# A two-layer backbone on one core: the first product of both MLPs by Strassen's algorithm, pairs of unit blocks at a time

## The chip, the cores and the metric

The kernel runs on one core of a Trainium2 chip. The metric is the time of one execution on the device, in microseconds (us). A kernel's time is the median over several executions; a profile is one further execution, recorded by the hardware. TensorE (PE) does the matrix products, with its weight loads (PEld) beside them; VectorE (DVE), ScalarE (ACT) and GpSimd (POOL) work on vectors; SyncE (SP) starts most transfers.

## The reference

Latent tokens (1024 of width 1024) and 256 context tokens pass two layers. Layer 0 mixes with a bidirectional state-space scan (SSD) beside neighbourhood attention (NA), layer 1 with a short gated convolution. Each layer ends in an MLP. This is the part that matters here:

```python
def sq_relu_mlp(h, w1, w2):
    return jnp.square(jax.nn.relu(h @ w1)) @ w2

...
        x = x + gate_a * y
        h = modulate(rmsnorm(x, norm_mlp_w[i]), shift_f, scale_f)
        x = x + gate_f * sq_relu_mlp(h, mlp_w1[i], mlp_w2[i])
    return rmsnorm(x, final_norm_w)
```

`w1` is 1024 x 4096 and `w2` 4096 x 1024, all in float32. `modulate` is `h * (1 + scale) + shift`, with vectors that come from a product of the conditioning vector with `mod_w`.

## The kernel before

Everything is kept transposed: channels on the 128 partitions, tokens along the free axis, in two halves t = 0 and 1 of 512 tokens. `x[t][k]` is the residual stream's block row k (of 8) of half t.

Each float32 product is three passes of a faster format. A value is split into a high part (a cast on ACT) and a low part (value minus high part, on DVE); the product is wh·xh + wh·xl + wl·xh, three matmuls of a 128 x 128 weight block with 512 columns, summed in PSUM. The class `Weights` does this for weights, in the order of a queue, `srcs`: a transfer on SP's queue into `wf` (128 x 512, two buffers), the cast to `wh` (L69) and the subtraction to `wl` (L70), four buffers each. `prefetch(n)` keeps n of them ready, `take` hands them out. `split` is the same pair of operations for activations. Each engine runs its instructions in the order in which they stand for it; a scheduler sets that order from the program's order and priorities when the kernel is built.

The program's stages are: norm and input projection (to about 120 us), SSD and NA with the output projection (to about 1220), MLP 0 (to about 1925), the short-convolution mixer (to about 2280), MLP 1 (to about 2990), final norm. In an MLP, the 32 blocks of 128 hidden units go in 8 groups of 4. For each block and half, `gemm` makes 24 matmuls (8 block rows of channels by three passes) into a PSUM bank `g`, ACT takes the relu and the high part of its square, DVE squares (L1094) and subtracts to get the low part (L1095). Then `proj` makes the second product of the group: for 8 output blocks and 2 halves 12 matmuls each into a `g`, and `resid` adds it to the stream, `x<-g,modv,x` (L883, on DVE). Five banks serve `g` and three `r`, for small sums.

The norm ahead of a stage has parts that are called as hooks inside the previous product: per half, a sum over partitions by a matmul with ones (`rstd`, L124, then small steps on DVE with a power on POOL, to `dg`), a broadcast by a matmul with `dg` (L141), and for each block row three operations: `xr` (L155, DVE), high part `hh` (L156, ACT), low part `hl` (L157, DVE). `acc` is the running sum of squares (L146 to L150). `mod_cols` computes the modulation vectors of layer 1, 128 columns in a step of 8 DVE operations (`macc`, L181 and L183): 48 steps, called as `between()` in MLP 0.

At the program's end, `fin1`, `fin2`, `fin3` are the final norm for three pieces of tokens (half 0, and two quarters of 256), with a scaling (L1193) and a transfer out for each block row.

## Time and profile before

| what | before |
|---|---|
| three runs, median (lowest to highest) | 3009.93 us (3008.55 to 3010.86) |
| profiled execution, its own time | 3005.5 us |
| its span (first to last instruction) | 3003.6 us |
| TensorE, mean granted clock | 0.997 of full |
| matmuls recorded | 14232 |
| busy: PE, PEld, DVE, ACT, POOL | 2940.2, 2416.9, 1739.0, 1042.9, 327.6 us |

The span leaves out about 2 us around the first and last instruction. The profiled execution is 4.4 us quicker than the median of the three timed runs. Busy time of the matmuls comes from modelled ends, since they are pipelined; the distance between starts tells the pace.

### The profile page before, as it was taken

How to read it: one execution, taken by the hardware profiler on the slowest of the kernel's cores; microseconds unless marked ns; L12 is line 12 of the kernel's file. 1: busy time of each engine (PE TensorE's matmuls, PEld its weight loads, DVE VectorE, ACT ScalarE, POOL GpSimd, SP SyncE). 2: the span in 40 equal slices, each digit the busy share in tenths (PEclk: the TensorE clock that was granted, in tenths of full speed). 3: DMA queues.
4: the chain of work that ended last, by engine and by line, in shares of the span. 5: the costliest groups of instructions: out<-in, count | busy, mean ns of one | idle time of the engine just before them, and what ended most of it. 6: DMA issues, size and time to landing. Idle time of an engine off the chain costs nothing.

```text
span 3003.6 us, 38877 instructions
## 1 busy us (share of the span) xinstructions
PE 2940.2 (98%) x14232; PEld 2416.9 (80%) x14232; DVE 1739.0 (58%) x3681; ACT 1042.9 (35%) x2006; POOL 327.6 (11%) x320
## 2 busy tenths in 40 slices
PE   8999999999999999999999999999999999999998
PEld 4888777777888778788888888788887888888886
DVE  6766758758998863755555554733336333333336
ACT  3544335446666642321212222422223222222222
POOL 1000024425545300000000000000000000000000
PEclk9999999999999999999999999999999999999999
DMA  7256765557776652223333331111111111111112
GB/s 215 88 193 205 252 164 149 161 147 186 203 177 167 180 174 62 67 88 90 90 91 91 89 90 55 36 57 50 43 56 43 50 50 50 47 48 50 47 49 78
DMA packets 333807, 317.09 MB, mean 106 GB/s; under 512 B 82544, under 2 KB 249456, under 8 KB 333616
## 3 DMA queue, kind: packets, MB, share of 16 engines
q1 hardware_dynamic: 331744, 311.98, 35.8%
q8 instruction: 113, 1.85, 0.2%
q10 hardware_dynamic: 1872, 2.62, 0.2%
q14 instruction: 78, 0.64, 0.1%
HBM read 254.24 MB, written 60.29 MB: 105 GB/s over the span
## 4 chain that ended last, share of the span: by engine, by line
PE 72%; DVE 4%; DMA 2%; issue 1%; ACT 1%; POOL 1%; SPq 0%; POOLq 0%; DVEq 0%; ACTq 0%
PE g L110 22%; PE g L111 22%; PE g L112 22%; PE v L1025 2%; PE r L999 1%; PE r L978 1%; PE r L979 1%; PE r L997 1%; DMA yf<-yna 0%; DMA yf<-yssd 0%; DVE P L985 0%; DVE PT L70 0%; DVE xr L155 0%; DVE hl L157 0%; DVE P L990 0%
## 5 line engine op out<-in xcount | busy, mean ns | idle before, releaser
L110 PE MATMUL g<-hh,wh 128*128 128x512 f32 (+1 forms) x2472 | 954.4, 387 | 3.1 <-ACT hh L69 0.8
L111 PE MATMUL g<-hl,wh 128*128 128x512 f32 (+1 forms) x2472 | 944.7, 383 | 2.3 <-DVE hl L157 2.0
L112 PE MATMUL g<-hh,wl 128*128 128x512 f32 (+1 forms) x2472 | 942.7, 382 | 2.1 <-DVE wl L70 2.0
L69 ACT CAST wh<-wf 128x512 fp32r<-128x512 f32 x442 | 274.9, 622 | 944.6 <-PE g L111 927.5
L112 PEld LDWEIGHTS g<-hh,wl 128*128 128x128 f32 x2472 | 465.0, 188 | 92.2 <-DVE wl L70 5.2
L111 PEld LDWEIGHTS g<-hl,wh 128*128 128x128 f32 x2472 | 465.5, 188 | 90.4 <-DVE hl L157 6.0
L110 PEld LDWEIGHTS g<-hh,wh 128*128 128x128 f32 x2472 | 464.9, 188 | 90.1 <-issue 1.7
L110 PE MATMUL g<-ah,wh 128*128 128x512 f32 (+1 forms) x1296 | 505.3, 390 | 0.4 <-ACT ah L69 0.3
L111 PE MATMUL g<-al,wh 128*128 128x512 f32 (+1 forms) x1296 | 501.7, 387 | 0.2 <-DVE al L70 0.2
L112 PE MATMUL g<-ah,wl 128*128 128x512 f32 (+1 forms) x1296 | 501.0, 387 | 0.0
L883 DVE SCALAR_TENSOR_TENSOR x<-g,modv,x 128x512 f32<-128x512 f32 (+1 forms) x300 | 222.7, 742 | 374.9 <-PE g L112 374.6
L70 DVE TENSOR_TENSOR wl<-wf,wh 128x512 fp32r<-128x512 f32 x442 | 308.3, 699 | 204.5 <-ACT wh L69 204.0
L110 PEld LDWEIGHTS g<-ah,wh 128*128 128x128 f32 x1296 | 243.5, 188 | 51.0 <-ACT ah L69 1.6
L111 PEld LDWEIGHTS g<-al,wh 128*128 128x128 f32 x1296 | 243.5, 188 | 50.1 <-DVE al L70 1.1
L112 PEld LDWEIGHTS g<-ah,wl 128*128 128x128 f32 x1296 | 243.4, 188 | 49.2
L1094 DVE TENSOR_TENSOR relu<-relu 128x512 f32<-128x512 f32 x128 | 88.2, 690 | 232.6 <-ACT ah L1093 232.6
L183 DVE SCALAR_TENSOR_TENSOR macc<-mw,sc,macc 128x128 f32<-128x128 f32 (+1 forms) x448 | 171.4, 383 | 11.1
L989 POOL TENSOR_SCALAR P<-P,mn 128x384 f32<-128x384 f32 (+1 forms) x128 | 154.8, 1210 | 191.1 <-DVE mn L988 140.6
L1091 ACT ACTIVATE relu<-g 128x512 f32<-128x512 f32 x128 | 76.1, 596 | 254.0 <-PE g L112 253.9
L128 POOL TENSOR_TENSOR rs<-ms,neghalf 128x4 f32<-128x4 f32 (+2 forms) x20 | 16.5, 827 | 1092.0 <-DVE ms L126 1090.5
L987 ACT ACTIVATE P<-P,mn 128x640 f32<-128x640 f32 (+1 forms) x128 | 103.1, 805 | 48.2 <-DVE P L985 46.9
L70 DVE TENSOR_TENSOR PT<-r,PT 128x256 fp32r<-128x256 f32 (+1 forms) x256 | 113.6, 463 | 1.9 <-ACT PT L69 1.0
(197 smaller groups left out, 2791.9 us busy)
## 6 DMA issues: line engine op xcount, KB each, us to landing
wf<-in_mlp_w SPq DMA_DIRECT2D x256, 256.0 KB
mw<-in_mod_w SPq DMA_DIRECT2D x64, 512.0 KB
wf<-in_in_w SPq DMA_DIRECT2D x90, 256.0 KB
mw<-in_mod_w SPq DMA_DIRECT2D x16, 1024.0 KB
wf<-in_out_w SPq DMA_DIRECT2D x48, 256.0 KB
wf<-in_sc_in SPq DMA_DIRECT2D x48, 256.0 KB
...
```

Source lines behind the costliest of these rows:

```text
L69: nc.scalar.copy(hi, src)
L70: nc.vector.tensor_sub(lo, src, hi.bitcast(F32))
L110: nc.tensor.matmul(ps, wh, xh, start=first and k == 0, stop=False)
L111: nc.tensor.matmul(ps, wh, xl, start=False, stop=False)
L112: nc.tensor.matmul(ps, wl, xh, start=False, stop=last and k == n - 1)
L183: nc.vector.scalar_tensor_tensor(acc, mw[:, k], sc[:, k, 0:1], acc, op0=OP.mult, op1=OP.add)
L883: nc.vector.scalar_tensor_tensor(xk, ps[:, :n], gate, xk, op0=OP.mult, op1=OP.add)
L987: nc.scalar.activation(P[:, w0:], P[:, w0:], AF.Exp, bias=mn[:, 1:2], scale=-1.0, accum_out=mn[:, 2:3])
L989: nc.gpsimd.tensor_scalar(P[:, w0:384], P[:, w0:384], mn[:, 3:4], None, op0=OP.mult)
L1025: nc.tensor.matmul(o, l, r, start=i == 0, stop=i == len(seq) - 1, skip_group_check=True)
L1091: nc.scalar.activation(r, ps, AF.Relu)
L1094: nc.vector.tensor_mul(r, r, r)
```

## The change

Per MLP, the hidden units are taken two blocks at a time, m = 0 to 15. Pair 0 is done as before. From pair 1 on the first product is one level of Strassen's algorithm in Winograd's form. The weights of a pair are a matrix of 2 x 2 quarters (block by half of the channels: a11, a12, a21, a22), the activations one of 2 x 2 quarters (half of the channels by half of the tokens). Seven products of quarters, each 4 block rows by three passes = 12 matmuls, replace eight. They need:

- sums of weight quarters, s1 = a21 + a22, s2 = s1 - a11, s3 = a11 - a21, s4 = a12 - s2, made on POOL (`add`) from the raw tiles `yf` into `xr`, then split like other weights (`entry`, a callable in `srcs`);
- sums of activation quarters, made once per MLP by `combine(k)` for k = 0 to 3: five POOL operations, three DVE sums, four splits, into T[0] to T[3]; their buffers are `sb` (three) and `relu` (two);
- sums of products: two are formed in PSUM by going on in the same bank (`x`, `y`), others by a copy on ACT (`kept`) that DVE adds when it makes the hidden values (`hidden` with a `part`).

The second product is `second(m)`, for each pair: 16 outputs of 6 matmuls and 16 `resid`, so that there are 256 per MLP in place of 128. The weights `w2` are laid out anew for it. PSUM in an MLP is now three banks `g`, two `r`, two `x`, one `y`. Half of the `mod_cols` steps of layer 1 move from MLP 0 to the mixer. At the program's start the transfers are reordered and the first three blocks of the input projection are interleaved over k.

```diff
     def mlp_srcs(l):
-        for g in range(8):
-            for f in range(4):
-                srcs.extend(halves(a["mlp_w1"][l, g * 4 + f], 8))
-            srcs.extend(a["mlp_w2"][l, g, b] for b in range(8))
...
+        def add(x, y, op):
+            t = np_.tile([128, 512], F32, name="xr", bufs=3).rearrange("p (k c) -> p k c", k=4)
+            nc.gpsimd.tensor_tensor(t, x, y, op=op)
+            return t
...
+        for m in range(1, 16):
+            srcs.extend(entry(m, x) for x in ("s2", "s1", "s3"))
+            if m < 15:
+                srcs.append(entry(m + 1, "a11"))
+            srcs.extend(entry(m, x) for x in ("a22", "s4"))
+            if m < 15:
+                srcs.append(entry(m + 1, "a12"))
+            srcs.extend(w2(m))
...
+        def hidden(m, f, t, ps, part=None):
+            r = Tmp()
+            ah, al = Act()
+            if part is None:
+                nc.scalar.activation(r, ps, AF.Relu)
+                nc.scalar.activation(ah, r, AF.Square)
+                nc.vector.tensor_mul(r, r, r)
+            else:
+                nc.vector.tensor_add(r, ps, part)
+                nc.vector.scalar_tensor_tensor(r, r, 0.0, r, op0=OP.max, op1=OP.mult)
+                nc.scalar.copy(ah, r)
+            nc.vector.tensor_sub(al, r, F(ah))
...
+        def combine(k):
+
+            whole = []
+            for t, i in ((0, k), (1, k), (1, k + 4), (0, k + 4)):
+                v = Tmp() if len(whole) == 3 else Sum()
+                nc.gpsimd.tensor_tensor(v, F(hs[t][i][0]), F(hs[t][i][1]), op=OP.add)
+                whole.append(v)
+            x, y, z, w = whole
+            nc.vector.tensor_sub(z, z, y)
+            nc.gpsimd.tensor_tensor(y, y, x, op=OP.subtract)
+            nc.vector.tensor_add(x, z, x)
+            nc.vector.tensor_sub(w, w, x)
+            for i, v in ((2, z), (1, x), (3, w), (0, y)):
+                if i:
+                    h_, l_ = (ap_.tile([128, 512], F32R, name=n, bufs=12) for n in ("ah", "al"))
+                else:
+                    h_, l_ = H1(k, 1)
+                split(h_, l_, v)
+                T[i][k] = h_, l_
...
+        combine(0)
+        x, p1 = begin1()
+        combine(1)
+        begin2(1, p1)
+        second(0, False, {3: lambda: combine(2), 7: lambda: combine(3)})
+        for m in range(1, 16):
+            product(x, T[1], False, True)
+            u2 = kept(x)
+            y = Y()
+            product(y, T[0], True, True)
+            product(x, T[2], False, True)
+            u3 = kept(x)
+            if m < 15:
+                x2, p1 = begin1()
+            product(x, T[3], False, True)
+            hidden(m, 1, 1, y, u3)
+            hidden(m, 1, 0, x)
+            product(y, B22, False, True)
+            hidden(m, 0, 1, y, u2)
+            between()
+            if m < 15:
+                begin2(m + 1, p1)
+                x = x2
+            second(m, m == 15)
+            between()
```

How the change moves instructions shows at three places. In the rows, `L883` and `L942` are the evictions of `resid` before and after, `L155`/`L158` and the other norm lines differ by the lines added above them.

DVE at the start of MLP 1, before: the first group's last hidden values and the first evictions of the second product.

```order
L1095 TENSOR_TENSOR al<-relu,ah 128x512
L70 TENSOR_TENSOR wl<-wf,wh 128x512 x2
L1094 TENSOR_TENSOR relu<-relu 128x512
L1095 TENSOR_TENSOR al<-relu,ah 128x512
L1094 TENSOR_TENSOR relu<-relu 128x512
L1095 TENSOR_TENSOR al<-relu,ah 128x512
L70 TENSOR_TENSOR wl<-wf,wh 128x512 x2
L1094 TENSOR_TENSOR relu<-relu 128x512
L1095 TENSOR_TENSOR al<-relu,ah 128x512
L883 SCALAR_TENSOR_TENSOR x_0_10470<-g,modv,x_0_10470 128x512
L883 SCALAR_TENSOR_TENSOR x_1_11596<-g,modv,x_1_11596 128x512
```

DVE at the start of MLP 1, after: `combine(1)` (L1216, L1218, L1219 are its sums, the `al` and `hl` rows its splits, `sb` and `relu` its buffers) and the first evictions.

```order
L1153 SCALAR_TENSOR_TENSOR relu<-relu 128x512
L1216 TENSOR_TENSOR sb<-sb 128x512
L942 SCALAR_TENSOR_TENSOR x_0_10470<-g,modv,x_0_10470 128x512
L1218 TENSOR_TENSOR sb<-sb 128x512
L70 TENSOR_TENSOR al<-sb,ah 128x512
L1219 TENSOR_TENSOR relu<-relu,sb 128x512
L70 TENSOR_TENSOR al<-sb,ah 128x512
L70 TENSOR_TENSOR hl_1_21405<-sb,hh_1_21404 128x512
L70 TENSOR_TENSOR al<-relu,ah 128x512
L942 SCALAR_TENSOR_TENSOR x_0_10472<-g,modv,x_0_10472 128x512
L942 SCALAR_TENSOR_TENSOR x_1_11596<-g,modv,x_1_11596 128x512
L942 SCALAR_TENSOR_TENSOR x_1_11598<-g,modv,x_1_11598 128x512
```

The first eviction now stands behind a sum of `combine(1)`, and the next one behind six more of its operations.

PE from MLP 0 to the mixer, before: the broadcast for half 0 (`r<-dg,ones`) with the last output of half 1 behind it, twelve matmuls in all, of which the first six stand here, ahead of the mixer's first gemm.

```order
L112 MATMUL g<-ah,wl 128x512
L141 MATMUL r<-dg,ones 128x512
L110 MATMUL g<-ah,wh 128x512
L111 MATMUL g<-al,wh 128x512
L112 MATMUL g<-ah,wl 128x512
L110 MATMUL g<-ah,wh 128x512
L111 MATMUL g<-al,wh 128x512
L112 MATMUL g<-ah,wl 128x512
```

PE from MLP 0 to the mixer, after: the last output's matmuls, the broadcast, the sums for half 1 (`r<-ones,acc`) and the mixer's first gemm (`hh`, `hl`).

```order
L1182 MATMUL g<-al,wh 128x512
L1183 MATMUL g<-ah,wl 128x512
L1181 MATMUL g<-ah,wh 128x512
L1182 MATMUL g<-al,wh 128x512
L1183 MATMUL g<-ah,wl 128x512
L144 MATMUL r<-dg,ones 128x512
L127 MATMUL r<-ones,acc 128x1 x4
L113 MATMUL g<-hh_0_18283,wh 128x512
L114 MATMUL g<-hl_0_18284,wh 128x512
L115 MATMUL g<-hh_0_18283,wl 128x512
```

The last output of six matmuls now stands ahead of the broadcast, and no product stands between it and the gemm.

DVE at the program's end, before, from the last eviction on (L150 the sums of squares, L1193 the scaling).

```order
L883 SCALAR_TENSOR_TENSOR x_1_11610<-g,modv,x_1_11610 128x256
L1193 SCALAR_TENSOR_TENSOR x_0_10478<-x_0_10478,vec,r 128x512
L150 TENSOR_TENSOR acc<-acc,sq 128x256
L1193 SCALAR_TENSOR_TENSOR x_0_10480<-x_0_10480,vec,r 128x512
L150 TENSOR_TENSOR acc<-acc,sq 128x256
L1193 SCALAR_TENSOR_TENSOR x_0_10482<-x_0_10482,vec,r 128x512
L126 TENSOR_SCALAR ms<-r 128x2
L1193 SCALAR_TENSOR_TENSOR x_0_10484<-x_0_10484,vec,r 128x512
L130 TENSOR_TENSOR nt<-rs 128x2
L1193 SCALAR_TENSOR_TENSOR x_1_11596<-x_1_11596,vec,r 128x256
```

DVE at the program's end, after, from the last eviction on (L153 and L1378 are the same operations; L133 to L139 the small steps of a scale).

```order
L942 SCALAR_TENSOR_TENSOR x_1_11610<-g,modv,x_1_11610 128x256
L133 TENSOR_TENSOR nt<-rs 128x2
L153 TENSOR_TENSOR acc<-acc,sq 128x256
L134 TENSOR_TENSOR nt<-nt,ms 128x2
L1378 SCALAR_TENSOR_TENSOR x_0_10472<-x_0_10472,vec,r 128x512
L135 TENSOR_SCALAR nt<-nt 128x2
L153 TENSOR_TENSOR acc<-acc,sq 128x256
L136 TENSOR_TENSOR rs<-rs,nt 128x2
L1378 SCALAR_TENSOR_TENSOR x_0_10474<-x_0_10474,vec,r 128x512
L139 TENSOR_SCALAR dg_26461<-ident,rs 128x128 x2
L153 TENSOR_TENSOR acc<-acc,sq 128x256
L1378 SCALAR_TENSOR_TENSOR x_0_10476<-x_0_10476,vec,r 128x512
```

More sums of squares and scalings of half 0 stand behind the last eviction now.

## Rows read from the trace of the kernel before

**Rows 1.** The page: busy time, and the chain that ended last.
```profile
PE 2940.2 (98%) x14232; PEld 2416.9 (80%) x14232; DVE 1739.0 (58%) x3681; ACT 1042.9 (35%) x2006; POOL 327.6 (11%) x320
...
PE 72%; DVE 4%; DMA 2%; issue 1%; ACT 1%; POOL 1%; SPq 0%; POOLq 0%; DVEq 0%; ACTq 0%
```

**Rows 2.** Windows: stretch, its length, busy us (instructions) by engine, clock, DMA.
```profile
20.00:30.00 10.00, 8.97 (x39) 3.87 (x40) 3.71 (x18) 0.55 (x2) 1.01 (x1) 0.83 1.17 303
1240.00:1920.00 680.00, 679.97 (x3047) 563.85 (x3046) 376.28 (x801) 155.81 (x257) 1.14 (x3) 1.00 0.28 83
1920.00:1940.00 20.00, 18.31 (x73) 12.19 (x72) 18.41 (x41) 9.40 (x15) 1.45 (x1) 1.00 0.11 40
2300.00:2980.00 680.00, 679.97 (x3025) 563.57 (x3024) 275.78 (x407) 162.43 (x269) 1.01 (x1) 1.00 0.15 48
```

**Rows 3.** Timeline of PE, end of the mixer: start, length, instruction.
```profile
2275.68 0.39 PE L111 MATMUL g<-al,wh 128*128 128x512 f32 x1
...
2278.85 0.39 PE L110 MATMUL g<-ah,wh 128*128 128x512 f32 x1
```

**Rows 4.** Groups of instructions by shape, DVE, 2320 to 2980 us.
```profile
L883 DVE SCALAR_TENSOR_TENSOR x<-g,modv,x 128x512 f32<-128x512 f32 x124 | 93.0, 750 | 184.0 <-PE g L112 184.0
L70 DVE TENSOR_TENSOR wl<-wf,wh 128x512 fp32r<-128x512 f32 x119 | 81.7, 687 | 73.4 <-ACT wh L69 73.4
L1094 DVE TENSOR_TENSOR relu<-relu 128x512 f32<-128x512 f32 x59 | 40.8, 692 | 133.7 <-ACT ah L1093 133.7
```

**Rows 5.** Groups by shape, ACT, 2320 to 2980 us.
```profile
L69 ACT CAST wh<-wf 128x512 fp32r<-128x512 f32 x119 | 74.4, 625 | 364.0 <-PE g L111 364.0
```

**Rows 6.** Groups by shape, POOL, whole span.
```profile
L722 POOL TENSOR_TENSOR E<-E,gt 128x512 f32<-128x512 f32 x32 | 43.0, 1345 | 80.3 <-ACT E L715 49.9 <-issue 13.8 <-DVE gt L720 10.0
...
L150 POOL TENSOR_TENSOR acc<-acc,sq 128x512 f32<-128x512 f32 x7 | 10.0, 1432 | 13.6 <-ACT sq L149 13.3
```

**Rows 7.** Timeline of POOL, SSD stage.
```profile
574.30 1.86 POOL L722 TENSOR_TENSOR E<-E,gt 128x512 f32<-128x512 f32 x1 [1.11 <-DVE gt L720]
578.24 1.40 POOL L722 TENSOR_TENSOR E<-E,gt 128x512 f32<-128x512 f32 x1 [2.08 <-ACT E L715]
583.55 1.28 POOL L722 TENSOR_TENSOR E<-E,gt 128x512 f32<-128x512 f32 x1 [3.91 <-ACT E L715]
```

**Rows 8.** Timeline of DVE over the same two moments.
```profile
574.33 0.68 DVE L70 TENSOR_TENSOR wl<-wf,wh 128x512 fp32r<-128x512 f32 x1
574.93 0.68 DVE L70 TENSOR_TENSOR ev<-g,ev 128x512 fp32r<-128x512 f32 x1
...
578.64 1.55 DVE L70 TENSOR_TENSOR wl<-wf,wh 128x512 fp32r<-128x512 f32 x1 [0.16 <-ACT wh L69]
```

**Rows 9.** Timeline of DVE, start of MLP 1.
```profile
2308.41 0.74 DVE L157 SCALAR_TENSOR_TENSOR hl<-xr,modv,hh 128x512 fp32r<-128x512 f32 x1
...
2313.12 1.28 DVE L1095 TENSOR_TENSOR al<-relu,ah 128x512 fp32r<-128x512 f32 x2
```

**Rows 10.** Timeline of PE, from MLP 0 to the mixer.
```profile
1916.20 1.05 PE L124 MATMUL r<-ones,acc 128*128 128x1 f32 x8
...
1923.12 1.02 PE L141 MATMUL r<-dg,ones 128*128 128x512 f32 x2
```

**Rows 11.** Timeline of DVE there, the scale's last step.
```profile
1920.96 0.88 DVE L136 TENSOR_SCALAR dg<-ident,rs 128x128 f32<-128x128 f32 x4
```

**Rows 12.** Timeline of DVE, end of the program.
```profile
2988.38 0.48 DVE L883 SCALAR_TENSOR_TENSOR x<-g,modv,x 128x256 f32<-128x256 f32 x1
...
2995.25 4.78 DVE L1193 SCALAR_TENSOR_TENSOR x<-x,vec,r 128x256 f32<-128x256 f32 x12
```

**Rows 13.** The tile macc: count, duration ns min/median/max, first and last start, forms.
```profile
L183 DVE SCALAR_TENSOR_TENSOR macc<-mw,sc,macc x448: 339/352/489, 115.5 to 1820.1; 128x128 f32<-128x128 f32 x112, 128x256 f32<-128x256 f32 x38
...
L181 DVE TENSOR_SCALAR macc<-mw,sc x64: 275/280/354, 115.0 to 1816.6; 128x128 f32<-128x128 f32 x48, 128x256 f32<-128x256 f32 x16
```

**Rows 14.** Timeline of PE, the in-projection's first gemms.
```profile
80.51 0.50 PE L110 MATMUL g<-hh,wh 128*128 128x512 f32 x1 [0.68 <-ACT u L573]
```

More of the change, by code (lines that the diff above doesn't have):

```diff
@@ L568, in body @@
             for i, (o, n) in enumerate(SEG):
-                for m, (_, ws) in enumerate(first):
-                    ps = G()
-                    gemm(ps[:, :n], ws, [(hh[k][:, o:o + n], hl[k][:, o:o + n]) for k in range(8)])
+                pss = [(R if i == 1 else G)() for _ in first]
+                run = [gemm_steps(ps[:, :n], ws, [(hh[k][:, o:o + n], hl[k][:, o:o + n]) for k in range(8)])
+                       for ps, (_, ws) in zip(pss, first)]
+                for k in range(8):
+                    for steps in run:
+                        next(steps)
+                for m, ps in enumerate(pss):
                     if m:
@@ new lines, in mlp @@
+                hidden(0, f, t, ps)
+                between()
+        W.prefetch(2)
+        T = [[None] * 4 for _ in range(4)]
+        def combine(k):
[12 more added lines that the diff above has]
+                    h_, l_ = (ap_.tile([128, 512], F32R, name=n, bufs=12) for n in ("ah", "al"))
+                else:
+                    h_, l_ = H1(k, 1)
+                split(h_, l_, v)
+                T[i][k] = h_, l_
@@ new lines, in mlp, with kept, begin1, begin2 @@
+        B11, B21, B22 = hs[0][:4], hs[0][4:], hs[1][4:]
+        X = lambda: pp.tile([128, 512], F32, name="x", tag="x", bufs=2)
+        Y = lambda: pp.tile([128, 512], F32, name="y", tag="y", bufs=1)
+        def kept(ps):
+            v = Sum()
+            nc.scalar.copy(v, ps)
+            return v
+        def begin1():
+            x = X()
+            product(x, B11, True, True)
+            return x, kept(x)
+        def begin2(m, p1):
+            z = G()
+            product(z, B21, True, True)
+            hidden(m, 0, 0, z, p1)
@@ L1137, in body @@
         tp = sbuf("tmp0", 1, st)
-        mods = mod_cols(tp, R, 1, range(0, 6144, 128), 128)
-        mlp(0, lambda: next(mods, None), n0, hooks={(6, 1, 0): {0: n1[0]}, (7, 1, 0): {0: n1[1]}})
+        mods = mod_cols(tp, lambda: R(), 1, range(0, 3072, 128), 128)
+        pm = mlp(0, lambda: next(mods, None), n0, hooks={(6, 1, 0): {0: n1[0]}, (7, 1, 0): {0: n1[1]}})
         for _ in mods:
             pass
+    pm.close()
+    stage_psum("ps3")
     ys = [[], []]
@@ L1146, in body @@
         tp = sbuf("tmp1", 1, st)
+        na1 = 0
+        mods = mod_cols(tp, R, 1, range(3072, 6144, 128), 128)
         for j in range(8):
@@ L1160, in body @@
                     W.prefetch(2)
+                    next(mods, None)
                 o = t * 512
@@ L1203, in body @@
     fin3(2)
+    pm.close()
     M0.close()
```

152 lines of the change are left out of this document (114 added, 38 removed).

## The prediction

> **What bounds the kernel now.** I read the page first: TensorE (PE) is busy 98% of the span and 72% of the chain that ended last, VectorE (DVE) 58%, GpSimd (POOL) 11% [rows 1]. Busy time can hide gaps, so next the windows: through the middle of either MLP PE is busy 679.97 of 680 us at a full granted clock, while DVE is busy 376 and 276 us [rows 2]. There PE is the only limit. The timeline gives its pace: 15 matmuls of 512 columns start from 2275.68 to 2278.85, 14 steps of 0.2265 us [rows 3] (the 0.39 us shown are pipelined lengths, not the pace). So inside an MLP a matmul less is worth 0.2265 us, as long as nothing new makes PE wait; and the other engines' slack says how much new work fits.
>
> **What is removed.** Block pairs 1 to 15 of each MLP do the first product with seven quarter products of 12 matmuls, 84 in place of 96; pair 0 stays. 12 x 15 x 2 = 360 matmuls x 0.2265 = **-81.5 us**. The second product has the same matmuls, in runs of 6 in place of 12.
>
> **What is added, in the steady pairs.** A pair is now 84 + 96 = 180 matmuls, 40.8 us of PE. DVE has per pair 16 evictions `x<-g,modv,x` of 0.750, 11 weight splits `wl` of 0.687, and 11 operations for the hidden values, two-input adds like L1094 at 0.692 [rows 4]: 12.0 + 7.6 + 7.6 = 27.2 us. POOL has four weight adds per pair; its nearest rows are additions of the same shape, 1.345 and 1.432 mean [rows 6], so 5.2 to 5.7 us, and even if DVE stood still for all of them it has 33 of 40.8 us. ACT has 11 casts of 0.625 [rows 5] and some eight other passes like them, about 12 us. Averages leave 8 us of cover a pair, so I take **0**. The cover is thin in one place: the first eviction of each pair's second product stands on DVE behind two hidden-value operations and a weight split, and PE has only three `g` banks to run ahead; by the rows it is done 2.8 us after PE begins that product, and the fourth output, which reuses that bank, asks for it after 3 x 6 x 0.2265 = 4.1 us. 1.3 us to spare; without them every us late costs 30 us in all (a rival, below). In the first five pairs of MLP 0 four `mod_cols` steps remain per pair, each 0.28 + 7 x 0.352 = 2.7 us [rows 13], so DVE has 38 to 44 of 40.8 us: **+3** (0 to 10). The 24 columns moved to the mixer come one per 144 matmuls (32.6 us), hidden behind PE: 0.
>
> **The start of each MLP.** This is the dear part. Before pair 1 may use T[1], `combine` must make sums of all four block rows: 20 POOL additions, 12 DVE sums, 16 splits. The order of DVE's instructions shows the last split that T[1] needs behind 38 operations with two inputs in SBUF and 10 with a PSUM input, counted from the last norm piece (2308.41 + 0.74 before [rows 9]) on, and 17 POOL additions stand before it too. Do POOL and DVE overlap? At 578 us they met: `wl` was issued 0.40 us after a POOL addition and took 1.55 us in place of 0.687, ending 0.55 us after POOL; at 574 POOL and `wl` were issued together and POOL took 1.86 in place of the 1.28 of a moment later [rows 7, 8], while a DVE operation that reads PSUM (`ev`) kept its 0.68 beside it. Here the trace agrees with the Trainium skill, "SBUF — State Buffer", section "Who interferes with whom": a DVE instruction with two SBUF inputs contends with a GpSimd instruction that reads SBUF, and one waits for the whole of the other. By that rule the two engines' times add; without it they could overlap, and the sum below would start from 29 instead of 45 us. By rows, added: 38 x 0.60 (start to start; two in 1.28 [rows 9]) + 17 x 1.28 = 44.6 us, from about 2311. In that time PE can run only the ten matmuls left of the fourth gemm, 24 for pair 1's first two products, and 11 of the 16 outputs of 6 (the rest wait for banks that are freed behind the splits): 100 x 0.2265 = 22.6 us. So PE stands **22 us**. Lower bound: POOL wholly hidden, 38 x 0.60 + 10 x 0.66 = 29.4, so 7 us; upper bound: the PSUM-reading ones not hidden behind POOL either, 51.2, so 29. The three `sb` buffers, which make a row's POOL additions wait for the row before it to be split, speak for the upper part. MLP 0 has ten `macc` operations more among them, 3.5 us: **26 us** (10 to 33). Such stops may also cost clock: after the waits of the kernel's start one 10 us slice shows 0.83 [rows 2].
>
> **The seams.** From MLP 0 to the mixer: before, the sum of squares (1916.20) and the broadcast (1923.12) lie 26 matmuls apart, and 12 more cover the first norm pieces [rows 10, 11]. With outputs of 6, ten matmuls remain between the sums and the first gemm, 2.3 us, against a chain that took 5.6 us to the scale (1921.84) and some 2 to 3 us for broadcast and first pieces; less the 1.7 us that PE already stood there in 20 us [rows 2], **+4.5** (2 to 8). The end: DVE now makes an eviction and a square sum per 1.36 us of PE, and falls behind, since each pair of them takes 0.66 + 0.60; the order puts seven scalings of 0.66, six sums of 0.34 and a chain after the last eviction, and all 16 final scalings of 0.40 behind the last chain. 7.3 + 2.8 + 6.4 + 3.6 (output) = 20.1 us from the last eviction to the end, against 2988.86 to 3003.6 = 14.7 now [rows 12]: **+6** (3 to 9). The kernel's start is reordered but waits for the same bytes; one wait of 0.68 us goes [rows 14]: **-1** (-3 to 1).
>
> **Sum.** -81.5 + 22 + 26 + 3 + 4.5 + 6 - 1 = -21 us. The profiled execution took 3005.5, so 2984.5. The median of the three runs, 3009.93, is 4.4 us above the profiled one, and I forecast on the median: **2989 us**.
>
> **Rivals.**
> *The start is cheap.* POOL's additions hide (stops of 7 and 10 us in place of 22 and 26): -81.5 + 7 + 10 + 3 + 4.5 + 6 - 1 = -52, 2958 us. For it: over the 32 additions L722 the mean is 1.345 against 1.28 alone, so most met no one [rows 6]. Against it: the row at 578. With the pairs' seams free as well it would be no lower than 2940.
> *The pairs stall.* Slower than before: DVE takes its instructions in order, and in each pair a weight split that waits for its cast, its transfer behind the next raw loads on SP, or POOL's chain s1, s2, s4, holds the first evictions. The spare is 1.3 us; each us beyond it is 30 us in all. At 0.7 us per pair the gain is gone, at 1.5 us per pair it is +24, 3034 us. For it: one more engine in the path of the weights, two raw buffers only for the second product. Against it: 8 us of cover per pair, and weights asked for two ahead.
> *A late clock.* The stops of 20 us drop the granted clock and PE stays slow for some slices; at half clock each 10 us so spent cost 5 us. Two starts: +5 to +15, near no change at the worst.
> *No change in effect.* The order shows 84 matmuls per pair, so the removal itself is certain; no chance is given to it.
>
> **How the numbers follow.** Main case (2970 to 3003) 0.50; cheap start (2940 to 2970) 0.24; pairs stall or the clock falls 0.26, of which half end within 6 us of before. The range reaches to the middle of the cheap start and takes in the mild stalls: 2950 to 3014; the main case's own is 2970 to 3003. A difference of 0.2% (6 us) is about what a measurement of this kernel can tell from no change. Faster by more: 0.50 + 0.24 + a part of the mild ones, less a bad main case: 0.76; within: 0.12; slower: 0.12.
>
> **What the profile of the changed kernel would show.** 360 matmuls less; 0.2265 us pace in the pairs; PE idle of some 20 us at each MLP start, released by `al` or `hl` splits of DVE, with POOL additions of 1.3 to 1.9 us and DVE splits over 1 us among them; idle below 0.3 us in every pair after the fifth; 4 to 6 us more idle at the seams. I am wrong if PE's idle at the two starts is under 20 or over 65 us together, if pairs 6 to 15 show more than 0.5 us each, or if the pace in runs of 6 is not 0.2265.

## The result and the profile after

The changed kernel takes 3028.69 us (median of 4 runs, 3026.72 to 3033.45) against 3009.24 before (4 runs, 3008.37 to 3010.86): a ratio of 1.0068 [1.0056, 1.0080]. It is slower, by 19.5 us, where I had forecast 21 us less. The profiled execution has a span of 3026.5 us.

The page after, in the order of [rows 1]:

```profile
PE 2892.9 (96%) x13860; PEld 2362.9 (78%) x13860; DVE 2119.9 (70%) x4177; ACT 1105.3 (37%) x2130; POOL 560.8 (19%) x480
...
PE 61%; DVE 10%; DMA 4%; issue 2%; ACT 1%; POOL 1%; SPq 0%; POOLq 0%; DVEq 0%; ACTq 0%
```

PE lost 372 records, and is busy 47 us less; DVE stands on the path for 10% of the span in place of 4%. To see where, I cut both kernels at the same places: the first matmul with `ones` for half 0 ahead of each norm. These are the windows of the kernel before, for MLP 0, mixer of layer 1, MLP 1 and the end (stretch and its length; busy us and instructions of PE, PEld, DVE, ACT and POOL; granted clock; share and GB/s of DMA):

```profile
1191.04:1916.20 725.16, 723.86 (x3236) 598.56 (x3237) 411.95 (x866) 176.82 (x290) 2.19 (x4) 1.00 0.27 81
1916.20:2272.64 356.44, 354.63 (x1556) 289.98 (x1557) 144.96 (x228) 91.21 (x146) 3.35 (x16) 1.00 0.14 48
2272.64:2976.16 703.52, 702.14 (x3106) 579.62 (x3106) 296.67 (x445) 174.50 (x287) 2.01 (x2) 1.00 0.15 48
2976.16:3003.60 27.44, 14.80 (x96) 12.47 (x95) 20.85 (x62) 3.22 (x8) 2.40 (x3) 0.76 0.44 154
```

And of the changed kernel, the same four, then a steady stretch of MLP 1 and four short ones:

```profile
1201.07:1930.46 729.39, 697.46 (x3037) 568.38 (x3038) 540.53 (x900) 208.20 (x352) 117.89 (x84) 0.98 0.21 64
1930.46:2298.71 368.25, 356.69 (x1578) 293.61 (x1576) 205.70 (x441) 90.45 (x146) 3.33 (x16) 0.98 0.25 78
2298.71:2996.02 697.31, 675.83 (x2941) 552.32 (x2941) 483.24 (x689) 204.12 (x346) 119.13 (x82) 0.99 0.15 47
2996.02:3026.50 30.48, 11.73 (x70) 9.27 (x68) 22.90 (x69) 4.89 (x12) 2.52 (x3) 0.74 0.39 138
...
2480.00:2960.00 480.00, 479.85 (x2117) 396.95 (x2116) 316.37 (x450) 130.09 (x223) 67.61 (x48) 1.00 0.16 51
...
70.00:80.00 10.00, 4.70 (x14) 3.81 (x15) 7.68 (x21) 3.70 (x8) 0.69 (x1) 0.66 0.00 0
1220.00:1240.00 20.00, 12.91 (x51) 10.53 (x50) 12.41 (x26) 6.85 (x11) 1.03 (x1) 0.83 0.14 39
1280.00:1300.00 20.00, 13.78 (x38) 9.43 (x39) 18.84 (x23) 6.62 (x11) 14.59 (x10) 0.66 0.05 14
2340.00:2360.00 20.00, 13.65 (x56) 10.31 (x55) 20.00 (x22) 7.26 (x13) 12.67 (x8) 0.88 0.18 53
```

A stage's length alone misleads, since outputs of 6 matmuls also move matmuls across the cuts. So I use the **excess**: the stage's time after, less its time before, plus 0.2265 us for each 512-column matmul that it lost, 0.12 for each 256-column one (eight start within 0.96 us at the end of the program), and less 0.075 for each small matmul of the 24 columns that it gained (a pair of them stretches a step of PE from 0.2265 to 0.37). MLP 0 lost 152 matmuls and 48 small ones, the mixer lost 28 and gained those 48, MLP 1 lost 168 and gained 3 narrow ones, the end lost 27 narrow ones. MLP 0: 729.4 - 725.2 + 34.4 + 3.6 = 42.3 (from unrounded times). Of it the first two columns show 31.9 - 1.3 = 30.6 us of PE idle, and the rest, 11.7, as matmuls that took longer, at a granted clock of 0.98. MLP 1: 31.5, of which 20.1 idle; the mixer 14.6, of which 9.7 idle; the end 6.3. The first stages, whose matmuls are the same, add 10.0, and 7.7 of it is there by the first transposes of `dtT`. Sum 104.6, less 81.7 for the matmuls: +22.9, the profiled difference.

The waits of PE at the start of MLP 0 (1200 to 1360), of MLP 1 (2290 to 2400), and in their later pairs (1360 to 1900, 2400 to 2990); us, times, longest:

```profile
PE r L127 <- DVE acc L153: 7.1, 1, 7.1
PE g L1181 <- DVE x L942: 6.7, 3, 2.8
PE g L1181 <- DVE relu L1152: 3.8, 2, 2.4
...
PE g L1181 <- DVE x L942: 6.2, 4, 3.9
PE g L1181 <- DVE relu L1152: 5.3, 1, 5.3
PE r L127 <- DVE acc L153: 3.5, 1, 3.5
...
PE g L1181 <- DVE relu L1152: 3.6, 5, 1.1
...
PE g L1181 <- ACT ah L1154: 1.0, 1, 1.0
```

The pairs run as forecast: PE is busy 479.85 of 480 us. Nearly all of the loss is at the starts and seams. In MLP 0 and at the mixer the largest single wait is not on the sums of the changed product but on the norm's; in MLP 1 the norm's 3.5 us come behind 5.3 on a hidden value (`relu`) and 3.9 on an eviction. The timeline of PE, with the idle time before each instruction:

```profile
75.30 1.19 PE L144 MATMUL r<-dg,ones 128*128 128x256 f32 x2 [5.96 <-DVE dg L139]
...
1230.41 1.87 PE L127 MATMUL r<-ones,acc 128*128 128x1 f32 x8 [7.08 <-DVE acc L153]
...
1936.85 1.13 PE L144 MATMUL r<-dg,ones 128*128 128x512 f32 x2 [3.00 <-DVE dg L139]
1943.92 1.87 PE L127 MATMUL r<-ones,acc 128*128 128x1 f32 x8 [5.95 <-DVE acc L153]
2312.88 1.05 PE L127 MATMUL r<-ones,acc 128*128 128x1 f32 x8 [3.46 <-DVE acc L153]
```

The granted clock falls behind such stops, to a mix of the 2.4 and the 1.2 GHz level: 0.66 in 70 to 80, 0.83 in 1220 to 1240, and 0.66 in 1280 to 1300, behind the shorter stops for `combine`. Two of the stretches of MLP 0 in which the lower level was granted throughout:

```profile
1228.67:1235.49 6.82, 5.08 (x16) 4.40 (x17) 3.46 (x12) 1.25 (x2) 1.03 (x1) 0.50 0.29 77
1276.45:1293.51 17.06, 11.34 (x26) 7.45 (x25) 14.75 (x18) 4.98 (x9) 12.60 (x9) 0.50 0.15 46
```

### The profile page after: what moved, and what is told of

Its sections match the earlier page's. It is cut to its first block, busy times and chain, and to the rows that moved or that the text cites. A ratio compares the mean times of both kernels' runs of the same rounds, so it can differ in the third digit from the quotient of the medians.

```text
span 3026.5 us, 38894 instructions
## 1 busy us (share of the span) xinstructions
PE 2892.9 (96%) x13860; PEld 2362.9 (78%) x13860; DVE 2119.9 (70%) x4177; ACT 1105.3 (37%) x2130; POOL 560.8 (19%) x480
## 3 DMA queue, kind: packets, MB, share of 16 engines
q1 hardware_dynamic: 331744, 311.98, 35.5%
## 4 chain that ended last, share of the span: by engine, by line
PE 61%; DVE 10%; DMA 4%; issue 2%; ACT 1%; POOL 1%; SPq 0%; POOLq 0%; DVEq 0%; ACTq 0%
PE x L1162 9%; PE g L1181 7%; PE g L113 7%; PE g L114 7%; PE g L1182 7%; PE g L115 7%; PE g L1183 7%; PE y L1162 4%; PE v L1084 2%; PE g L1162 2%; DMA mw<-in_mod_w 1%; DVE wl L70 1%; DVE macc L186 1%; PE r L1058 1%; DVE x L942 1%
## 5 line engine op out<-in xcount | busy, mean ns | idle before, releaser
L113 PE MATMUL g<-hh,wh 128*128 128x512 f32 (+1 forms) x1488 | 576.6, 389 | 6.2 <-ACT hh L159 4.6
L114 PE MATMUL g<-hl,wh 128*128 128x512 f32 (+1 forms) x1488 | 565.8, 380 | 3.1 <-DVE hl L160 2.7
L115 PE MATMUL g<-hh,wl 128*128 128x512 f32 (+1 forms) x1488 | 564.2, 379 | 1.1 <-DVE wl L70 0.9
L942 DVE SCALAR_TENSOR_TENSOR x<-g,modv,x 128x512 f32<-128x512 f32 (+1 forms) x558 | 410.0, 742 | 188.1 <-PE g L1183 122.4
L1181 PE MATMUL g<-ah,wh 128*128 128x512 f32 (+1 forms) x1036 | 407.6, 394 | 29.1 <-DVE x L942 13.7
L114 PEld LDWEIGHTS g<-hl,wh 128*128 128x128 f32 x1488 | 282.9, 190 | 54.3 <-DVE hl L160 6.6
L113 PEld LDWEIGHTS g<-hh,wh 128*128 128x128 f32 x1488 | 282.7, 190 | 54.2 <-ACT hh L159 5.6
L115 PEld LDWEIGHTS g<-hh,wl 128*128 128x128 f32 x1488 | 282.4, 190 | 51.4 <-DVE wl L70 1.9
L1181 PEld LDWEIGHTS g<-ah,wh 128*128 128x128 f32 x1036 | 196.2, 190 | 79.5 <-DVE x L942 21.5
L1162 PE MATMUL x<-ah,wh 128*128 128x512 f32 x360 | 141.5, 393 | 2.2 <-ACT wh L69 1.2
L1162 PE MATMUL x<-al,wh 128*128 128x512 f32 x360 | 140.5, 390 | 0.3 <-DVE al L70 0.3
```

What stands on the lines that cost most here:

```text
L113: nc.tensor.matmul(ps, wh, xh, start=first and k == 0, stop=False)
L114: nc.tensor.matmul(ps, wh, xl, start=False, stop=False)
L115: nc.tensor.matmul(ps, wl, xh, start=False, stop=last and k == n - 1)
L942: nc.vector.scalar_tensor_tensor(xk, ps[:, :n], gate, xk, op0=OP.mult, op1=OP.add)
L1162: nc.tensor.matmul(ps, w[:, k], x, start=start and k == 0 and i == 0, stop=stop and k == 3 and i == 2, skip_group_check=True)
L1181: nc.tensor.matmul(ps[:, :n], wh, ah, start=k == 0, stop=False)
```

## The experiments

My first theory was that `combine` makes most of the loss, by DVE's time; the rivals were the contention of POOL and DVE, the three `g` banks, and the order at starts and seams. All runs in one table: the median, the ratio to the kernel before with its interval (none for a single run), and from the profile the delay at `dtT` and the excess of each stage. The stretch from `dtT` to the first cut, with the same instructions in all, took 1096 to 1107 us in single profiles (1096 before, 1099 changed), so that I compare stages with stages and runs with runs.

| kernel | us | ratio | dtT | MLP 0 | mixer | MLP 1 | end |
|---|---|---|---|---|---|---|---|
| changed | 3028.7 | 1.0068 [1.0056, 1.0080] | 7.7 | 42.3 | 14.6 | 31.5 | 6.3 |
| no_combine | 2986.8 | one run | 8.1 | 13.8 | 16.1 | 9.7 | 7.0 |
| dve_sums | 3029.3 | 1.0073 [1.0058, 1.0088] | 7.8 | 40.6 | 14.7 | 28.5 | 6.4 |
| two_plain | 3049.3 | 1.0127 [1.0109, 1.0145] | 8.1 | 49.0 | 15.5 | 34.0 | 6.3 |
| mods_late | 3033.6 | one run | 8.6 | 40.8 | 15.8 | 31.9 | 6.3 |
| four_g | 3032.2 | one run | 8.0 | 42.5 | 14.7 | 29.4 | 8.3 |
| norm_order | 3030.1 | 1.0071 [1.0055, 1.0088] | 8.4 | 35.5 | 18.4 | 31.4 | 6.2 |
| five_g_start | 3019.7 | 1.0044 [1.0027, 1.0061] | 7.7 | 34.6 | 15.7 | 27.9 | 6.8 |
| old_banks | 3029.9 | 1.0075 [1.0060, 1.0090] | 4.4 | 41.9 | 14.7 | 31.2 | 6.3 |
| old_start | 3024.9 | 1.0051 [1.0035, 1.0068] | 1.5 | 42.4 | 16.1 | 32.5 | 6.3 |
| tail | 3029.8 | one run | 6.8 | 41.4 | 17.1 | 31.4 | 6.2 |
| sq2 | 3033.5 | 1.0083 [1.0068, 1.0098] | 7.6 | 41.6 | 15.8 | 31.6 | 4.5 |
| last_joint | 3018.6 | 1.0032 [1.0021, 1.0044] | 7.8 | 40.9 | 8.4 | 31.8 | -0.3 |
| all_cures | 3028.5 | 1.0064 [1.0046, 1.0082] | 4.0 | 31.2 | 18.3 | 34.1 | 7.2 |
| spread | 3011.1 | 1.0008 [0.9997, 1.0018] | -0.3 | 28.1 | 17.2 | 22.0 | 6.3 |
| all_joint | 2979.8 | 0.9905 [0.9889, 0.9922] | -0.9 | 21.7 | 7.5 | 15.8 | -1.0 |
| all_joint_prio | 2979.7 | 0.9905 [0.9890, 0.9919] | -0.5 | 24.1 | 7.2 | 15.8 | -0.3 |
| all_right | 2981.1 | 0.9915 [0.9902, 0.9929] | -1.3 | 26.6 | 8.5 | 19.1 | -0.2 |
| five_g_end | 2981.8 | 0.9914 [0.9901, 0.9927] | -1.5 | 25.6 | 3.8 | 17.0 | -1.2 |

**What does combine cost?** no_combine leaves out the sums of hidden blocks: the products read the quarters themselves.

```diff
 def combine(k):
-    whole = [] ...
+    T[0][k], T[1][k], T[2][k], T[3][k] = hs[0][k], hs[0][k + 4], hs[1][k], hs[1][k + 4]
```

> The changed kernel with combine left out: T[0] to T[3] are taken straight from the quarters of the normalised activations, so no sums of activations are made and the MLPs' values are not the reference's. From the sums of half 0 ahead of one stage to those ahead of the next, MLP 0 took 725 us before and 729 after, MLP 1 703.5 and 697. Theory 'sums': the DVE and POOL work of combine is what PE stands for; then MLP 0 falls to 690 to 703 and MLP 1 to 664 to 676 us. Rival 'order': most of the stop is the norm of half 1, whose small matmuls now stand elsewhere among PE's; then both fall by less than 15 us.

MLP 0 loses 28.5 us and MLP 1 21.8: 50.3, where I had priced the two stops at 26 + 22. But 13.8 and 9.7 of excess stay in the MLPs with no sums at all. The two MLPs as windows of no_combine:

```profile
1207.54:1908.50 700.96, 689.68 (x3037) 567.16 (x3038) 510.88 (x872) 198.62 (x336) 84.55 (x64) 0.99 0.22 67
2278.30:2953.81 675.51, 668.73 (x2940) 550.74 (x2941) 455.06 (x661) 194.50 (x330) 86.92 (x62) 0.99 0.16 48
```

PE stands 11.3 and 6.8 us there, against 31.9 and 21.5 in the changed kernel. So 35.4 of the 50.3 are idle time of PE that goes with the sums; the other 15 are matmuls that took longer behind it. PE's waits of this kernel, 1200 to 1360 and then 2285 to 2400:

```profile
PE r L127 <- DVE acc L153: 6.0, 1, 6.0
...
PE r L127 <- DVE acc L153: 2.8, 1, 2.8
PE g L113 <- ACT hh L159: 1.6, 1, 1.6
```

The norm's wait is still there; `L1181 <- DVE x` is gone.

**Is it POOL beside DVE?** dve_sums makes POOL's sums in `combine` on DVE.

```diff
-nc.gpsimd.tensor_tensor(v, F(hs[t][i][0]), F(hs[t][i][1]), op=OP.add)
+nc.vector.tensor_tensor(v, F(hs[t][i][0]), F(hs[t][i][1]), op=OP.add)
```

> The changed kernel with combine's 20 POOL operations per MLP given to DVE. Theory 'port': DVE and POOL wait for each other whenever both read two operands in SBUF, so their times add; a POOL operation costs 1.3 to 1.7 us of the pair's time and 0.6 on DVE, so each MLP's start gets shorter by 10 to 18 us, 20 to 36 us in all. Rival 'overlap': POOL's operations ran beside DVE and the wait was for the number of DVE operations or for the three sb buffers; then 20 more on DVE (12 us per MLP) make it 0 to 24 us slower.

Timeline of DVE in the changed kernel, start of MLP 1:

```profile
2346.15 0.68 DVE L1150 TENSOR_TENSOR relu<-relu 128x512 f32<-128x512 f32 x1
2346.75 1.79 DVE L70 TENSOR_TENSOR wl<-wf,wh 128x512 fp32r<-128x512 f32 x1
...
2349.66 1.77 DVE L1218 TENSOR_TENSOR sb<-sb 128x512 f32<-128x512 f32 x1
```

of POOL there:

```profile
2346.30 1.68 POOL L1217 TENSOR_TENSOR sb<-sb 128x512 f32<-128x512 f32 x1 [1.83 <-DVE sb L1216]
2349.21 1.67 POOL L1213 TENSOR_TENSOR relu<-hh,hl 128x512 f32<-128x512 f32 x1 [1.23 <-DVE al L1155]
...
2361.83 1.28 POOL L1217 TENSOR_TENSOR sb<-sb 128x512 f32<-128x512 f32 x1 [1.23 <-DVE sb L1216]
```

and of DVE in dve_sums:

```profile
2347.28 0.68 DVE L1213 TENSOR_TENSOR sb<-hh,hl 128x512 f32<-128x512 f32 x1
2347.88 0.68 DVE L1150 TENSOR_TENSOR relu<-relu 128x512 f32<-128x512 f32 x1
2348.49 0.68 DVE L1213 TENSOR_TENSOR sb<-hh,hl 128x512 f32<-128x512 f32 x1
```

The contention is real: where the two meet, POOL takes 1.67 for 1.28 and DVE 1.79 for 0.68. This agrees with the Trainium skill, "SBUF — State Buffer", section "Who interferes with whom", by which a DVE instruction with two inputs in SBUF contends with a GpSimd instruction that reads SBUF. But taking it away gives nothing in the run (MLPs -1.7 and -3.0, the run +0.6). Each meeting delays DVE by 1.1 us, some 12 of them 13 us; 20 sums more on DVE at 0.60 from start to start cost 12. The gain of 20 to 36 didn't come, nor a price on top: the run lies at the lower edge of the rival's 0 to 24. DVE works without a pause in the changed kernel (20.00 of 20 us in 2340 to 2360) and nearly so in dve_sums (18.55 there, 19.19 in 2360 to 2380), so that its queue, whoever fills it, is the likely limit.

**More cover?** two_plain leaves pair 1 as before too, and puts whole `combine` calls between outputs of pairs 0 and 1 and behind a block of pair 1, so that far more matmuls lie beside them. mods_late takes the column steps out of the start of MLP 0. four_g gives `g` a fourth bank.

```diff
-second(0, False, {3: lambda: combine(2), 7: lambda: combine(3)})
+second(0, False, {3: lambda: combine(0), 11: lambda: combine(1)})   # two_plain; then pair 1 in full
...
-                if b % 4 == 3 and t == 1:
+                if m > 1 and b % 4 == 3 and t == 1:     # mods_late; its between() in pair 0 goes too
...
-"g", bufs=3 / "r", bufs=2
+"g", bufs=4 / "r", bufs=1     # four_g
```

> The changed kernel with pairs 0 and 1 of each MLP done plainly and Strassen's form from pair 2 on; combine's four parts are spread over pair 0's second product and pair 1's products. It has 24 matmuls more (5.4 us) and 312 matmuls, 70 us of PE, beside the 45 to 50 us of DVE that the sums keep busy. Theory 'sums without cover': with combine left out the two MLPs were 50 us shorter, so with cover for them 2 x (25 - 2.7) = 35 to 45 us are won: MLP 0 about 707 and MLP 1 about 678 us. Rival 'the sums cost wherever they stand', since a DVE that runs late frees PSUM banks late in any second product: under 15 us.

> The changed kernel with the modulation columns of layer 1 starting at pair 2, not at pair 0. Theory: MLP 0 stands 10 us longer than MLP 1 in its start because the columns' 2.7 us each stand among the sums; MLP 0 falls from 729 to 719 to 724 us. Rival: they only move, since MLP 0 has four per pair either way; 727 or more.

> The changed kernel with four g banks and one r bank in the MLPs. Theory 'bursts': each of the four combines, twice, lets PE run ahead by 1.36 us more before it stands; 5 to 11 us less over both MLPs. Rival 'sum': the stop is set by DVE's whole work before T[1], the banks only move it: under 3 us.

None gains in the run. mods_late takes 1.5 us from MLP 0 where I expected 5 to 10, the fourth bank changes MLP 0 by 0.2 and MLP 1 by -2.1. And two_plain is 20 us slower than the changed kernel: 5.4 are its 24 matmuls more, 9.2 are excess in the MLPs, and the rest lies ahead of MLP 0, where the two don't differ (9.4 in its profile). Its timeline at the start of MLP 1, on DVE, ACT and PE:

```profile
2416.36 0.69 DVE L1221 TENSOR_TENSOR sb<-sb 128x512 f32<-128x512 f32 x1 [1.18 <-POOL sb L1220]
...
2429.72 1.74 DVE L70 TENSOR_TENSOR al<-relu,ah 128x512 fp32r<-128x512 f32 x1
...
2431.50 0.60 ACT L1151 ACTIVATE relu<-g 128x512 f32<-128x512 f32 x1 [1.94 <-DVE al L70]
...
2432.15 0.80 PE L1184 MATMUL g<-ah,wh 128*128 128x512 f32 x1 [7.38 <-ACT relu L1151]
```

Cover in sum is not what is short there. From 2416.36 on DVE works without a pause for 15 us on the sums and splits of `combine`, while three banks with 6 matmuls each let PE run ahead 3 x 6 x 0.2265 = 4.1 us. And `combine`'s fourth sum lies in a buffer of the hidden values' `relu`: ACT can't begin the next hidden value before DVE has split it. PE stands 7.38 us behind that chain.

**The norm at an MLP's start.** The order of PE's instructions in the traces: between the broadcast of half 0 and the sums of half 1 lay 62 matmuls in MLP 0 (26 in MLP 1), now 39 (12); from these sums to the broadcast of half 1, 12 (16), now 45 (48). So PE asks for the sums before DVE has them, the 7.08 and 3.46 above. The new pool of three `g` and two `r` banks is opened just there. norm_order changes the order alone, by the priority and by the place where the sums are called; five_g_start keeps the old pool, with five `g`, until the four gemms of pair 0 are done.

```diff
-with tc.high_priority(offset=200):
+with tc.high_priority(offset=200) if t == 0 else ExitStack():     # norm_order
-gemm(ps, ws[f], hs[t])                        # norm_order; nrm[2 + f]() stood behind
+gemm(ps, ws[f], hs[t], {0: nrm[2], 5: nrm[3]} if f and not t else {})
...
-pst.close(); pp = psum(f"psm{l}", 1, pm)      # at the start of the MLP
+switch()                                      # five_g_start: the same, ahead of combine(0)
```

> The changed kernel with the sums of half 1 of each norm called without the raised priority, so that PE has them behind 62 matmuls after the broadcast of half 0 as before, and not behind 39, and the broadcast of half 1 sooner behind them. Theory 'order': PE stands 7.1 us and 3.5 us at these sums ahead of the MLPs and 5.9 us ahead of the mixer, and the clock falls with it; 10 to 22 us are won. Rival 'backlog': DVE is the limit there whatever PE does first, the stops move to the gemms behind; less than 5 us.

> The changed kernel with the banks of the stages before (five g, three r) until the first four gemms of an MLP are issued; the change to three g, two x and one y comes behind them. The order on PE is then as before: the sums of half 1 stand behind 62 matmuls and the broadcast 13 behind them. Theory 'banks set the order': each MLP stands 5 to 8 us less at its start, 10 to 16 us in all. Rival 'backlog': DVE's sums take over, as where only the order was put back; less than 4 us.

five_g_start has the old counts again (62 and 12, 26 and 16), the wait is gone, MLP 0 gains 7.7 and MLP 1 3.6, and the run 9 us (7 by the ratios). norm_order gains 6.8 in MLP 0, nothing in MLP 1, and loses 3.8 in the mixer: no gain in the run.

**The kernel's start.** The change interleaves the first gemms of the in-projection, with the outputs of the second stretch of tokens in `r` banks, and reorders loads. old_banks undoes the first, old_start both.

```diff
-pss = [(R if i == 1 else G)() for _ in first] ...     # interleaved
+ps = G(); gemm(ps[:, :n], ws, ...)                     # one after the other
...
-four xt1 loads, all behind k == 3                     # old_start as well
+xt1 load behind each k
```

> The changed kernel with the first three blocks of the input projection as before: one after the other, with g banks for the second stretch of tokens; the new order of the transfers stays. Theory 'banks': the second stretch takes r banks behind the broadcast for the context, so PE waits 5.96 us for its scale and runs the next matmuls at a lower clock; 7 to 9 us are won. Rival 'transfers': the new order of the loads has made the norm later; 0 to 2 us.

> The changed kernel with the whole start as before: the transfers' order and the first three blocks of the input projection. The transposes of dtT begin at 94.9 us before, at 102.6 after, at 99.3 with the blocks alone put back. Theory: blocks and transfers cost 3 to 4 us each, so 94 to 96 us here and 6 to 8 us less in all. Rival: the stretch behind gives it back, as the blocks alone moved the run by nothing; within 2 us of the changed kernel.

`dtT` comes 3.3 and 6.2 us earlier; the run of old_start is 3.8 us shorter (5 by the ratios), that of old_banks is not.

**The seams and the end.** tail, sq2 and last_joint all go at the last pair: tail takes another order of outputs in MLP 0, sq2 a second buffer for the squares, last_joint gives pairs 14 and 15 one second product in runs of 12, as before the change. In last_joint (and all_joint, all_joint_prio) the quarters of the last pair's weights come in another order, so that the product is another; number and kind of the operations are the same.

```diff
-order += [(b, *seg) for seg in segs for b in range(2, 8)]
+order += [(b, *seg) for seg in segs for b in range(0 if len(segs) == 2 else 2, 8)]   # tail
...
-sumsq(np_, accs[t][:, o:o + n], k, xk, n)
+sumsq(np_, accs[t][:, o:o + n], k, xk, n, bufs=2)      # sq2
...
-second(m, m == 15)
+second([14, 15], True) if m == 15 else second([m], False)     # last_joint; nothing for m == 14
```

> The changed kernel with the last second product of MLP 0 in another order: all eight outputs of half 0 first, then all eight of half 1, so that two more outputs (2.7 us) lie between the last eviction of half 0 and the mixer. From the sums of half 0 ahead of the mixer to those ahead of MLP 1 the changed kernel took 368.2 us, 356.4 before. Theory 'too little cover': 2.5 to 6 us less. Rival 'DVE's backlog': the sums of half 1 wait for DVE there (5.9 us), which stays; less than 1.5 us.

> The changed kernel with two buffers in place of one for the squares that feed the norm's running sum. Theory 'chain': with outputs of 6 matmuls an eviction comes every 1.36 us, and eviction, square and sum pass one buffer after another in 1.4 to 2.0 us, so the sums come late (PE stands 7.1, 5.9 and 3.5 us for them ahead of the two MLPs and the mixer); two buffers let the squares run ahead: 8 to 15 us less, of it 4 to 8 in the stage from MLP 0's end to MLP 1's. Rival 'DVE is full there': less than 3 us.

> The changed kernel with one second product for pairs 14 and 15 together: outputs of 12 matmuls and 16 evictions in place of 32 at the end of each MLP, as before the change. Theory 'runs of 6': evictions and square sums at twice the rate per matmul keep DVE behind at the end of an MLP, and too few matmuls lie between the norm's steps; the stage from the sums ahead of the mixer to those ahead of MLP 1 falls from 368 to 357 to 361 us and the end from 30.5 to 27 to 29, 9 to 14 us in all. Rival: the columns moved to the mixer, or DVE's load there, cost it; less than 3 us.

Only last_joint helps: seam 14.6 to 8.4, end 6.3 to -0.3, the run 10 us. It restores 26 matmuls between sums and broadcast, where the changed kernel has 10. tail has 19 there, but PE still stands 5.95 us at the sums of half 1, directly behind the broadcast, as its rival said; sq2 wins 1.8 us at the end and is no faster as a run.

**Cures together.** all_cures is two_plain, norm_order, mods_late's rule and old_banks. spread has the old start as a whole, and makes `combine` in six single steps, one between two outputs, with the sums of `T[0]` made again later and a buffer `wsum` for the fourth sum.

```diff
-            if n_ in mid:
-                mid[n_]()
+            for _ in range(mid.get(n_, 0)):
+                next(cg, None)                 # cg: chain of combine(0..3), a generator with yields
...
-second(0, False, {3: ..., 11: ...})
+second(0, False, {i: 1 for i in range(16)})
```

> The changed kernel with two plain pairs per MLP, the columns from pair 2 on, the sums of half 1 without raised priority and the input projection's first blocks as before. If the parts add: two plain pairs -35 to -45, columns -5, order of the norm -5, banks -3: about 2975 to 2985 us, faster than before by about 1%. Rival: they share one backlog of DVE, and the sum is no better than the two plain pairs alone, 2985 to 2995.

> The kernel with the start as before, the columns from pair 2 on, the norm's sums of half 1 without raised priority, two plain pairs, and combine cut in single steps: one step behind each output of pair 0's and two behind each gemm of pair 1, and the sums for T[0], made again on POOL, behind pair 1's outputs. All products as in the changed kernel from pair 2 on. Theory 'bursts': PE stands because a combine holds DVE for 10 to 12 us in one piece, and three g banks let PE run ahead 4.1 us only, wherever it stands (two plain pairs with whole combines won nothing); in steps of 0.6 to 1.3 us it hides. Then MLP 0 takes 700 to 712 and MLP 1 675 to 685 us, 2980 to 2995 in all. Rival 'DVE's sum': the work has no room even there; MLP 1 stays above 692, 3010 or more.

all_cures wins nothing as a run, where I expected 2975 to 2985. In the MLPs spread differs from it only in `combine`: single steps, at other places, a buffer of its own for the fourth sum, and two sums more per block row. MLP 0 goes from 31.2 to 28.1, MLP 1 from 34.1 to 22.0, and the run to the time before the change. That is less than expected: MLP 0 took 717.9 us, MLP 1 690.5 and the run 3011.1, where the theory said 700 to 712, 675 to 685 and 2980 to 2995, and the rival, DVE's sum, 3010 or more. So pieces and places count in MLP 1, though the sum of work grew, and in MLP 0 they are worth 3 us; steps, places and buffer were not tried apart, and the rival is not excluded. all_joint adds five_g_start and last_joint (and drops norm_order) and is 31 us faster than spread, more than the 9 and 10 that the two gave alone; no run takes that apart. all_joint_prio keeps norm_order's priority, all_right puts the quarters right, and five_g_end also opens a pool with five `g` banks ahead of the last second product.

```diff
+pm.close(); stage_psum(f"pse{l}")     # five_g_end
 second([14, 15], True)
```

> The spread kernel (start as before, columns from pair 2, two plain pairs, sums in single steps) with normal priorities, five g banks until the gemms of pair 1 are issued and the joint second product of pairs 14 and 15. The spread kernel ran 3011 us. If the seams at both ends of an MLP are what is left: MLP 0 700 to 710, mixer 358 to 362, MLP 1 677 to 685, 2978 to 2990 us in all, about 0.8% faster than before. Rival: DVE's whole work in the first 80 us of an MLP stays the bound; 2998 or more.

> The same with the norm's sums of half 1 called without raised priority. If only the order on PE matters, which the five banks already set, within 3 us of all_joint; if the priority also moves DVE's small steps behind other work, 3 to 8 us slower.

> All cures together, with the last pair's weight quarters in the order of its products: start as before, columns from pair 2, two plain pairs with five g banks, combine in single steps, joint second product of pairs 14 and 15. The same operations as all_joint, which took 2979.75 us; one transfer and one split of the last pair stand elsewhere. If nothing waits for them: 2975 to 2985 us, about 0.9% faster than the kernel before; if the last pair waits for the quarter's late transfer, up to 6 us more.

> The kernel all_right with five g and three r banks again before the joint second product of the last two pairs, in place of after it. The stage from the sums ahead of the mixer to those ahead of MLP 1 took 356.4 us before and 368.6 in all_right. Theory 'banks set the order on PE': with the banks there, the sums and the broadcast of half 1 stand 24 matmuls behind the broadcast of half 0 and 8 behind these, not 12 and 48; the stage falls to 359 to 363 us and the run to 2972 to 2977. Rival 'DVE's backlog' behind the evictions: the stage stays at 366 or more.

all_right is 0.85% faster than before, 26 us, with the quarters in their place. five_g_end brings the mixer's stage from 368.6 to 363.9 us, close to the 359 to 363 expected and short of the rival's 366 and more: in this profile the banks set that part of the seam. Its run is no shorter, 2981.8, where 2972 to 2977 was expected. Its windows for MLP 0, mixer, MLP 1:

```profile
1196.20:1905.30 709.10, 690.07 (x3020) 564.08 (x3020) 531.32 (x889) 205.30 (x348) 123.02 (x88) 0.99 0.22 67
1905.30:2269.20 363.90, 361.06 (x1605) 296.61 (x1605) 202.43 (x429) 91.04 (x146) 2.92 (x16) 1.00 0.25 77
2269.20:2951.70 682.50, 670.21 (x2938) 548.55 (x2938) 474.62 (x669) 202.33 (x345) 123.09 (x86) 0.99 0.16 48
```

PE stands 19.0, 2.8 and 12.3 us there, against 31.9, 11.6 and 21.5 in the changed kernel.

## Why the prediction was wrong, by its steps

**Removed matmuls, -81.5**: right, 81.7 by the counts, at the pace of [rows 3]. **Steady pairs, 0, and the first pairs, +3**: right. Waits in the later pairs are 3.6 us in MLP 0, 2.8 of them by 1510, and 1.0 in MLP 1; the rival in which every pair stalls did not come. Idle below 0.3 us in every pair after the fifth did not quite come either: 0.8 us stand at 1794 and 1.0 in the last pair of each MLP.

**The stops for `combine`, 22 + 26**: as a sum right, 21.8 + 28.5, but in part by luck. PE's idle time that goes with the sums is 14.7 and 20.7 us, 35 where the working had 48; the other 15 are longer matmuls, which it held for a rival (the clock). Of the working, the contention is right as a row and wrong as a cause: without it the stop is about as long, since DVE gets the work instead.

**The end, +6**: right, 6.3. Two small slips stand in that working: seven scalings and six sums at the prices named are 6.7 us, not 7.3, and 20.1 less 14.7 is 5.4, not 6. From the end of the last eviction to the end of the program the forecast had 20.1 us; DVE's rows of the changed kernel give 3005.65 + 0.47 to 3026.5, 20.4, with all 16 final scalings behind the last chain:

```profile
3005.65 0.47 DVE L942 SCALAR_TENSOR_TENSOR x<-g,modv,x 128x256 f32<-128x256 f32 x1
...
3017.24 6.35 DVE L1378 SCALAR_TENSOR_TENSOR x<-x,vec,r 128x256 f32<-128x256 f32 x16
```

**What failed** is the list of what is at the starts and seams, not a price on it:
- *The start of each MLP* was priced as if only `combine` stood there. The norm's sums and broadcast of half 1 kept no cover, by the order, though nothing in the diff touches them; with the clock after the stops 13.8 and 9.7 us remain beside `combine`, 20 more than the +3. five_g_start gives 11.3 of it back.
- *The seam, +4.5* (2 to 8): 14.6. The ten matmuls between sums and broadcast were counted rightly. But half 1 comes next: its sums stand directly behind that broadcast, with no matmul between (5.95 us of wait), where 24 lay before. Runs of 6 make 6.2 of it (last_joint), banks some 4.7 (five_g_end).
- *The kernel's start, -1*: +7.7. I took the reorder for neutral, since it "waits for the same bytes". The rows show PE at 75.30 behind the norm's `dg`, not behind bytes, 5.96 us, and a clock of 0.66 there. The other 2.3 us of the first stages are within what they vary by.

The clock was a rival, at +5 to +15 for two starts. It came true, beside the main case and not in its place: 11.7 and 11.4 us of longer matmuls (the excess less the idle) in the two MLPs, restarts after waits included, and 4.8 in the mixer's stage. No run sets the clock alone apart, but the trace of the changed kernel grants the lower level for 23.9 us of MLP 0 (PE busy in 16.4), 13.7 of the mixer's stage (8.4) and 20.5 of MLP 1 (15.6), that of the kernel before for none of them. At half the pace that is some 8, 4 and 8 us, an estimate. These are parts of the misses below, not added to them. The misses add up: 20.5 (MLP starts) + 10.1 (seam) + 8.7 (start) + 2.3 (the rest of the first stages) + 2.3 (`combine`) + 0.3 (end) = 44, the difference between -21 and +22.9.

None of the signs that I had named for being wrong came: idle at the two starts is 47 us, between the 20 and 65 named (27.2 of the 160 from 1200 on, 20.2 of the 110 from 2290 on), the pairs are quiet and the pace is right. They asked after what I had priced, and the loss was beside it.

**Open**: 26 and 17 us of excess that remain in the MLPs of the best kernels; why the stretch behind `dtT` varies by 11 us between profiles; and so whether old_banks is worth its 3.3 us.
